# Moving operands at a pitch of 1280 bytes, and small copies on ScalarE, in a two-layer hybrid decoder trunk

## The chip, the core and the metric

The kernel runs on one core of a Trainium2 chip. The core has five engines that run their own streams of instructions and wait for each other on semaphores: TensorE (PE, matmul, with its weight loads shown as PEld), VectorE (DVE), ScalarE (ACT), GpSimd (POOL) and SyncE (SP), which here issues the DMAs. The metric is the device time of one execution in microseconds.

## The reference

Each of two layers is a half-step feed-forward block, a mixer, and a second half-step feed-forward block:

```
x = x + 0.5 * swiglu(rmsnorm(x, norm_ffn1[l]), w_ffn1_gu[l], w_ffn1_down[l])
m = mixer(rmsnorm(x, norm_mix[l]), states, w_in[l], ...)
x = x + m
x = x + 0.5 * swiglu(rmsnorm(x, norm_ffn2[l]), w_ffn2_gu[l], w_ffn2_down[l])
...
# mixer
q, k, v, g, a_lr, z, xbc, dt_raw, gate_a, gate_b = split(u @ w_in)
o_gla = gla_chunked(q, k, v, log_a, gla0)          # gated linear attention
xbc = silu(causal_dwconv(xbc, conv0))              # 4 taps, old rows from conv0
y, ssm_new = ssd_chunked(xs, dt, A, B, C, ssm0)    # h <- decay * h + dS, y_off = C . h
m = sigmoid(gate_a) * (o_gla @ w_proj_gla) + sigmoid(gate_b) * (y @ w_proj_ssm)
return m @ w_out, new states
```

There are 256 prompt tokens and 8 samples of 4 tokens, so 288 columns; the model width is 1024, the feed-forward width 2816, and the mixer has 32 state heads of 64 x 128 in 4 groups that share B and C. All of it is in 32-bit floats, and a sample's states come from memory and go back to it.

## The kernel before

Activations are held transposed, features on the partitions and the 288 columns along the free axis. A product is made of three matmuls, to keep 32-bit accuracy: weights and activations are each split into a high part in the matmul's format and the rest (wh and wl, xh and xl). `weights` (line 174) loads a block of 128 output features (wr) on the SP queue, `split` makes wh on ScalarE (line 165) and wl on VectorE (line 171). `mm3` (line 181) then runs, for each 128 rows of the contraction, wh times xh (line 184) and wh times xl (line 185), and after that wl times xh (line 187): 24 matmuls for 1024 rows. The moving operands are the normed input (xh and xl, nine buffers each, given out in turn), the feed-forward's inner activations (hh and hl), and in the mixer oh and ob (the input of w_out) and yh and yb (the input of the state branch's projection). wr has four buffers, wh and wl three each. All are of 288 floats, 1152 bytes, per partition and tile.

The order of the instructions on each engine isn't that of the code: the framework's scheduler sets it when the kernel is built. The addresses are given out by the framework too.

The mixer's second half, `ssd`, is a generator of stages that lie among blocks of the input projection. `conv` copies a block's columns into a buffer beside the old rows of the samples (line 873, GpSimd) and does the four taps (lines 876 to 878); `conv_last` saves the last rows (lines 897 and 899, GpSimd). `stage_pack` makes, for one group of heads, c4, C of the samples four times with a mask (line 928, GpSimd), and b4, a packed copy of B (`pack`, line 143, GpSimd). `stage_group` spreads c4 over the partitions with a matmul (line 939), copies it into cbd (line 942, ScalarE), and forms the products of B and C (lines 956 to 958). `stage_t` transposes a head pair's states (line 993, VectorE) and then decays them (line 998, GpSimd, eight instructions of 128 x 128 for each of 16 head pairs). `stage_h` multiplies C by the states (line 1009). `stage_y` adds the new part to the states and stores them. The POOL instructions run in one queue in the scheduler's order, so c4 can stand behind decays.

Of the kernel before, what the change touches and what calls it, by code (L numbers as in the profile page):

```python
# [23 lines left out]
NT = SEQ + NSAMP  # L24
FFN = 2816
KF = 22
# [15 lines left out]
H2_BUFS = 2  # L42
# [55 lines left out]
def tile_hybrid_step(  # L98
# [42 lines left out]
    def pack(eng, out, src):  # L141

        eng.tensor_copy(out=out.rearrange("p (r c i) -> p r c i", r=4, c=4),
                        in_=bcast(src.rearrange("p (r i) -> p r i", i=8), 2, 4))
# [4 lines left out]

    cbd = cst.tile([128, 2 * 516], F32, name="cbd")  # L150
    cz = cbd[:, 0:528].rearrange("p (a b) -> p a b", a=2)
# [61 lines left out]
    def params(l, n1):  # L213
        pa = t1()[:, 0:128]
        rows = [(norm_mix[l], 16), (norm_ffn2[l], 24), (gla_norm[l], 32),
                (ssm_norm[l], 40), (conv_b[l], 56), (norm_final, 80)]
        ds = tmp.tile([16, 2], F32, name="ds", tag="ds")
        for a, r0 in rows:
            n = a.shape[0] // 128
            nc.sync.dma_start(out=pa[r0:r0 + n], in_=a.rearrange("(r c) -> r c", c=128))  # L220
        nc.sync.dma_start(out=ds, in_=d_skip[l].rearrange("(j h) -> j h", h=2))
        V.tensor_copy(out=pa[0:16].rearrange("p (h q) -> p h q", h=2), in_=bcast(ds, 2, 64))
        pb = t1()[0:96, 0:128]
        nc.sync.dma_start(out=pb, in_=conv_w[l].rearrange("i (r c) -> (i r) c", c=128))
        p = pst()
        tr(p[:, 0:88], pa[0:88], 88)
        o = tmp.tile([128, 88], F32, name="prm", tag="prm", bufs=2)
        A.activation(out=o, in_=p[:, 0:88], func=AF.Copy)
        p = pst()
        tr(p[:, 0:96], pb, 96)  # L230
        cw = tmp.tile([128, 96], F32, name="cw", tag="cw", bufs=1)

        A.activation(out=cw, in_=p[:, 0:96], func=AF.Copy, scale=0.5)
        V.tensor_scalar(out=o[:, 32:80], in0=o[:, 32:80], scalar1=0.5, scalar2=None, op0=ALU.mult)
        a32 = tmp.tile([32, 2], F32, name="a32", tag="a32", bufs=2)
        nc.sync.dma_start(out=a32[:, 0:1], in_=dt_bias[l].rearrange("(h o) -> h o", o=1))
# [44 lines left out]
    def xpair():  # L281
        return (res.tile([128, NT], F32R, name="xh", tag="xh", bufs=9),
                res.tile([128, NT], F32R, name="xl", tag="xl", bufs=9))
# [8 lines left out]
    def ffn(norm, w_gu, w_dn, nxt, setup=False):  # L292
        with tc.tile_pool(name="ffn", bufs=1) as fp:
            hh = fp.tile([128, KF, NT], F32R, name="hh")
            hl = fp.tile([128, KF, NT], F32R, name="hl")
# [282 lines left out]
    def gla(l, P, W, norm, X, renorm, dtc, dalt, o8):  # L578
        with tc.tile_pool(name="gla", bufs=1) as gp:
            G.memset(cbd[:, 0:528], 0.0)  # L580
# [281 lines left out]
    def ssd(l, P, W, X, yf, dtm, ac, dec3, eAm, decs, mse, acd, ysq, scf, cbufs, yr, yblk, proj):  # L862
# [3 lines left out]
        with tc.tile_pool(name="ssd", bufs=1) as sp_:  # L866
            def conv(pg, cb, tag, bufs):
# [5 lines left out]
                G.tensor_copy(out=sb[:, :, 0:3], in_=scf[:, 0:24, cb].rearrange("p (s t) -> p s t", t=3))  # L873
# [34 lines left out]

            G.memset(cbd, 0.0)
# [14 lines left out]
            def stage_pack(g):  # L924
# [3 lines left out]
                G.tensor_tensor(out=c4, in0=bcast(Cf[:, sp], 1, 4), in1=bcast(C["qm"], 2, 32), op=ALU.mult)  # L928
                b4 = sp_.tile([128, 128], F32, name="b4", tag="b4", bufs=3)
                pack(G, b4, Bf[:, sp])  # L930
                R["gp", g] = Bf, Cf, c4, b4

            def stage_group(g):

                Bf, Cf, c4, b4 = R.pop(("gp", g))


                p = pst()
                T.matmul(p[:, 0:128], lhsT=C["id4"], rhs=c4.rearrange("p b t -> p (b t)"), start=True, stop=True)
                for a in range(4):  # L940
                    rows = slice(32 * a, 32 * a + 32)
                    A.activation(out=cbd[rows].rearrange("p (h x) -> p h x", x=516)[:, :, 0:512].rearrange(
                        "p h (k c) -> p h k c", c=32)[:, :, :, 8 * a:8 * a + 4],
                        in_=p[rows, 0:128].rearrange("p (k h t) -> p h k t", h=2, t=4), func=AF.Copy)
# [21 lines left out]
                ms = sp_.tile([128, 4, 32], F32, name="msm", tag="msm", bufs=2)  # L966
                G.tensor_tensor(out=ms, in0=mse[:, 4 * g:4 * g + 4], in1=bcast(cbs, 1, 4), op=ALU.mult)
# [18 lines left out]
            def stage_t(j):  # L986
# [14 lines left out]
            def stage_h(hg):  # L1001
# [9 lines left out]
                yos = sp_.tile([128, 2, 4, 32], F32, name="yos", tag="h1", bufs=3)  # L1011
# [4 lines left out]
            def stage_x(j):  # L1016
# [5 lines left out]
                pack(G, x4, xs[:, sp])  # L1022
# [36 lines left out]
            def stage_y(j):  # L1059
# [18 lines left out]
                if j % 2 == 0:  # L1078
                    R["so", j // 2] = sp_.tile([128, 2, 128], F32, name="so", tag="h1", bufs=3)
# [29 lines left out]
            stage_group(0)  # L1109
            yield 1  # L1110
            stage_x(1)
            stage_t(1)
            stage_mask(0)
            yield 1
            stage_m(0)
            stage_h(0)
            yield 1
            for j in range(16):
# [52 lines left out]
    for l in range(DEPTH):  # L1171
# [40 lines left out]
        with tc.tile_pool(name="fin", bufs=1) as op:  # L1212
            if l == DEPTH - 1:
                yo = op.tile([128, 3, D], F32, name="yo")
                rt = op.tile([128, 3], F32, name="rt")
# [46 lines left out]
```

## Time and profile before

| | us |
|---|---|
| median of 3 executions | 1842.87 |
| lowest, highest | 1842.05, 1844.18 |
| the profiled execution, its own time | 1842.29 |
| its span | 1840.5 |

| engine | busy in the span | instructions |
|---|---|---|
| PE | 98% | 14304 |
| DVE | 68% | 2091 |
| ACT | 56% | 1850 |
| POOL | 20% | 549 |

The span is what the profiler shows between the first and the last instruction; 1.8 us of the execution lie around it. Matmuls are pipelined, and one's shown duration (about 297 ns for the main ones) overlaps the next, so their pace is read from start to start. An engine's share is a mean over stages: GpSimd works almost only in the two mixers.

### The profile page before, as it was taken

To read this page: it belongs to the slowest core of one execution; us is meant where nothing else is said; L and a number is where in the kernel's file an instruction comes from. 1 tells how busy PE (TensorE), PEld (TensorE's weight loads), DVE (VectorE), ACT (ScalarE), POOL (GpSimd) and SP (SyncE) were. 2 spreads that over 40 slices of the span, in tenths; PEclk is the share of its full clock that TensorE was granted. 3 is DMA by queue.
4 is the path that set the end of the run, shared out by engine and by line. 5 is a ranking of instruction groups with operands and counts; after the bars stand their busy time and mean duration, and the time that the engine had idled before them with its cause. 6 is when DMAs were issued, how large, how long until landed. Compare 5 with 4: busy or idle time off the path is not lost.

```text
span 1840.5 us, 36290 instructions
## 1 busy us (share of the span) xinstructions
PE 1798.1 (98%) x14304; PEld 1738.7 (94%) x14304; DVE 1259.7 (68%) x2091; ACT 1023.8 (56%) x1850; POOL 376.3 (20%) x549
## 2 busy tenths in 40 slices
PE   8999999989999999999999999999899999999998
PEld 8999999889889999999999999998888999999997
DVE  6555577679898767555565556777798987665554
ACT  6444476566667646444454445665766765454443
POOL 1000000046786500000000000000577781000000
PEclk9999999999999999999999999999999999999999
DMA  7555654866687655555555555568667776555552
GB/s 217 164 168 158 164 149 125 266 183 181 190 225 221 191 168 173 163 170 161 170 164 163 165 160 161 144 177 241 174 190 214 216 209 179 170 166 162 163 163 90
DMA packets 613118, 325.59 MB, mean 177 GB/s; under 512 B 17090, under 2 KB 607858, under 8 KB 612948
## 3 DMA queue, kind: packets, MB, share of 16 engines
q1 hardware_dynamic: 612900, 323.15, 61.0%
q8 instruction: 112, 1.84, 0.4%
q14 instruction: 58, 0.48, 0.1%
q10 hardware_dynamic: 48, 0.13, 0.0%
HBM read 293.01 MB, written 30.22 MB: 176 GB/s over the span
## 4 chain that ended last, share of the span: by engine, by line
PE 52%; DVE 3%; ACT 2%; DMA 2%; POOL 1%; issue 1%; DVEq 0%; SPq 0%; POOLq 0%; ACTq 0%
PE psg L184 16%; PE psg L185 16%; PE psg L187 16%; DMA wr<-in_w_in_dram 1%; POOL st L998 1%; DVE wl L171 1%; PE pst L147 1%; ACT wh L165 1%; DMA out_dram<-st 0%; DVE cacc L878 0%; PE yo L1009 0%; PE pst L1067 0%; PE pst L1092 0%; PE pst L807 0%; PE gyo L798 0%
## 5 line engine op out<-in xcount | busy, mean ns | idle before, releaser
L165 ACT ACTIVATE wh<-wr 128x1024 fp32r<-128x1024 f32 (+1 forms) x498 | 518.6, 1042 | 509.9 <-PE psg L185 391.0
L184 PE MATMUL psg<-xh,wh 128*128 128x288 f32 x2704 | 739.4, 299 | 4.9 <-ACT cbuf L872 2.4
L185 PE MATMUL psg<-xl,wh 128*128 128x288 f32 x2704 | 735.0, 297 | 0.1
L171 DVE TENSOR_TENSOR wl<-wr,wh 128x1024 fp32r<-128x1024 f32 (+1 forms) x496 | 596.0, 1203 | 145.3 <-ACT wh L165 143.3
L184 PEld LDWEIGHTS psg<-xh,wh 128*128 128x128 f32 x2704 | 508.0, 188 | 13.6 <-ACT cbuf L872 2.8
L185 PEld LDWEIGHTS psg<-xl,wh 128*128 128x128 f32 x2704 | 508.1, 188 | 3.8 <-issue 0.9
L187 PE MATMUL psg<-xh,wl 128*128 128x288 f32 x2704 | 417.9, 297 | 3.5 <-DVE wl L171 3.4
L187 PEld LDWEIGHTS psg<-xh,wl 128*128 128x128 f32 x2704 | 379.1, 189 | 7.6 <-DVE wl L171 5.6
L998 POOL TENSOR_SCALAR st<-st,decs 128x128 f32<-128x128 f32 x256 | 237.7, 945 | 35.8 <-DVE sT L993 17.7
L184 PE MATMUL psg<-hh,wh 128*128 128x288 f32 x704 | 190.3, 296 | 0.0
L185 PE MATMUL psg<-hl,wh 128*128 128x288 f32 x704 | 189.9, 295 | 0.0
L380 POOL MEMSET cbuf<- 128x3 f32 x4 | 0.3, 108 | 654.4 <-DVE t L331 654.4
L185 PEld LDWEIGHTS psg<-hl,wh 128*128 128x128 f32 x704 | 132.7, 188 | 0.0
L184 PEld LDWEIGHTS psg<-hh,wh 128*128 128x128 f32 x704 | 132.4, 188 | 0.1
L311 DVE TENSOR_TENSOR t<-t,psg 128x288 f32<-128x288 f32 x88 | 40.0, 454 | 134.9 <-ACT wh L165 122.8
L187 PE MATMUL psg<-hh,wl 128*128 128x288 f32 x704 | 109.3, 296 | 0.0
L308 DVE TENSOR_TENSOR t<-psg,rr 128x288 f32<-128x288 f32 x88 | 40.2, 457 | 90.5 <-PE psg L187 90.5
L187 PEld LDWEIGHTS psg<-hh,wl 128*128 128x128 f32 x704 | 99.0, 188 | 0.0
L878 DVE SCALAR_TENSOR_TENSOR cacc<-cbuf,cw,cacc 128x312 f32<-128x312 f32 x144 | 78.9, 548 | 12.2 <-ACT cacc L876 11.8
L184 PE MATMUL psg<-oh,wh 128*128 128x288 f32 x256 | 69.7, 299 | 0.0
L184 PE MATMUL psg<-yh,wh 128*128 128x288 f32 x256 | 69.7, 299 | 0.0
L185 PE MATMUL psg<-ob,wh 128*128 128x288 f32 x256 | 68.9, 295 | 0.0
(317 smaller groups left out, 2248.3 us busy)
## 6 DMA issues: line engine op xcount, KB each, us to landing
wr<-in_w_ffn_gu_dram SPq DMA_DIRECT2D x176, 512.0 KB
wr<-in_w_in_dram SPq DMA_DIRECT2D x160, 512.0 KB
wr<-in_w_ffn_down_dram SPq DMA_DIRECT2D x64, 448.0 KB
wr<-in_w_ffn_down_dram SPq DMA_DIRECT2D x32, 512.0 KB
st<-in_state_ssm_dram SPq DMA_DIRECT2D x64, 256.0 KB
out_dram<-st SPq DMA_DIRECT2D x64, 256.0 KB
wr<-in_w_proj_ssm_dram SPq DMA_DIRECT2D x32, 512.0 KB
gst<-in_state_gla_dram SPq DMA_DIRECT2D x32, 256.0 KB
```

What stands on the lines that cost most here:

```text
L147: T.transpose(out, in_, ident[0:k, 0:k])
L165: A.activation(out=h, in_=raw, func=AF.Copy)
L171: V.tensor_tensor(out=lo, in0=raw, in1=h, op=ALU.subtract)
L184: T.matmul(out, lhsT=h[:, k], rhs=xh[k], start=start and k == 0, stop=False)
L185: T.matmul(out, lhsT=h[:, k], rhs=xl[k], start=False, stop=False)
L187: T.matmul(out, lhsT=lo[:, k], rhs=xh[k], start=False, stop=stop and k == n - 1)
L308: V.tensor_tensor(out=t, in0=pg, in1=r, op=ALU.mult)
L311: V.tensor_tensor(out=h, in0=t, in1=pu, op=ALU.mult)
L380: G.memset(cbufs[i][:, 0:3], 0.0)
L878: V.scalar_tensor_tensor(out=acc, in0=buf[:, i:i + NCV], scalar=w[i], in1=acc, op0=ALU.mult, op1=ALU.add)
L998: G.tensor_scalar(out=st[:, r], in0=st[:, r], scalar1=decs[:, n:n + 1], scalar2=None, op0=ALU.mult)
```

## The change

Five things change. The tiles xh, xl, hh and hl get 320 floats of which 288 are used, so that their pitch is 1280 bytes; a pad of 256 bytes and a longer rt shift what is allocated. The copy of the old conv rows, the packing and the masked C go from GpSimd to ScalarE. The decays leave `stage_t` for a stage of their own, `stage_decay`, an iteration later. The spread of C gets the bank that the product of C and the states uses (tag acc) and stands at the end of `stage_group`, which itself goes behind `stage_x(1)`. And some tiles move or lose a buffer (cbd, cz, msm, prm, h1) to make room.

```diff
+NTP = 320
...
     def pack(eng, out, src):
 
-        eng.tensor_copy(out=out.rearrange("p (r c i) -> p r c i", r=4, c=4),
-                        in_=bcast(src.rearrange("p (r i) -> p r i", i=8), 2, 4))
+        out, in_ = out.rearrange("p (r c i) -> p r c i", r=4, c=4), bcast(src.rearrange("p (r i) -> p r i", i=8), 2, 4)
+        if eng is A:
+            A.activation(out=out, in_=in_, func=AF.Copy)
+        else:
+            eng.tensor_copy(out=out, in_=in_)
...
-    cbd = cst.tile([128, 2 * 516], F32, name="cbd")
-    cz = cbd[:, 0:528].rearrange("p (a b) -> p a b", a=2)
...
     def xpair():
-        return (res.tile([128, NT], F32R, name="xh", tag="xh", bufs=9),
-                res.tile([128, NT], F32R, name="xl", tag="xl", bufs=9))
+        return (res.tile([128, NTP], F32R, name="xh", tag="xh", bufs=9)[:, 0:NT],
+                res.tile([128, NTP], F32R, name="xl", tag="xl", bufs=9)[:, 0:NT])
...
-            hh = fp.tile([128, KF, NT], F32R, name="hh")
-            hl = fp.tile([128, KF, NT], F32R, name="hl")
+            fp.tile([128, PAD], F32, name="pad")
+            hh = fp.tile([128, KF, NTP], F32R, name="hh")[:, :, 0:NT]
+            hl = fp.tile([128, KF, NTP], F32R, name="hl")[:, :, 0:NT]
...
-                G.tensor_copy(out=sb[:, :, 0:3], in_=scf[:, 0:24, cb].rearrange("p (s t) -> p s t", t=3))
+                A.activation(out=sb[:, :, 0:3], in_=scf[:, 0:24, cb].rearrange("p (s t) -> p s t", t=3), func=AF.Copy)
...
-                G.tensor_tensor(out=c4, in0=bcast(Cf[:, sp], 1, 4), in1=bcast(C["qm"], 2, 32), op=ALU.mult)
+                for b in range(4):
+                    A.activation(out=c4[:, b], in_=Cf[:, sp], func=AF.Copy, scale=C["qm"][:, b:b + 1])
                 b4 = sp_.tile([128, 128], F32, name="b4", tag="b4", bufs=3)
-                pack(G, b4, Bf[:, sp])
+                pack(A, b4, Bf[:, sp])
...
-                p = pst()
-                T.matmul(p[:, 0:128], lhsT=C["id4"], rhs=c4.rearrange("p b t -> p (b t)"), start=True, stop=True)
...
-                ms = sp_.tile([128, 4, 32], F32, name="msm", tag="msm", bufs=2)
-                G.tensor_tensor(out=ms, in0=mse[:, 4 * g:4 * g + 4], in1=bcast(cbs, 1, 4), op=ALU.mult)
+                ms = mse[:, 4 * g:4 * g + 4]
+                G.tensor_tensor(out=ms, in0=ms, in1=bcast(cbs, 1, 4), op=ALU.mult)
+
+
+                p = ps.tile([128, 128], F32, name="pc", tag="acc", bufs=1)
+                T.matmul(p[:, 0:128], lhsT=C["id4"], rhs=c4.rearrange("p b t -> p (b t)"), start=True, stop=True)
...
+
+            def stage_decay(j):
                 for hf in range(2):
                     st = R["st", j][hf]
                     for r in range(4):
...
             stage_t(0)
-            stage_group(0)
             yield 1
             stage_x(1)
+            stage_group(0)
             stage_t(1)
             stage_mask(0)
             yield 1
             stage_m(0)
+            stage_decay(0)
             stage_h(0)
...
                 if j + 2 < 16:
                     stage_t(j + 2)
+                if j + 1 < 16:
+                    stage_decay(j + 1)
```

On PE, at the spread of C of the first group in layer 0, this stands before (L939 is the spread, L147 a transpose, L956 to L958 the products of B and C, L187 matmuls of a weight block, L1009 the product with the states):

```order
L187 MATMUL psg<-xh,wl 128x288 x3
L939 MATMUL pst<-c_4405,call 128x128
L147 MATMUL pst<-call,bcf 128x128 x2
L147 MATMUL pst<-call,b_4407 128x128
L956 MATMUL pst<-bcf 128x256
L957 MATMUL pst<-bcf 128x128
L958 MATMUL pst<-bcf,b_4407 128x32
L187 MATMUL psg<-xh,wl 128x288 x5
L1009 MATMUL yo<-sT,cbd 32x64 x32
```

and this after (L967 is the spread, into pc, L151 a transpose, L954 a product, L1016 the product with the states, L185, L186 and L188 the lines of `mm3`); the two transposes of B stand 21 rows ahead of L967 and the two large products (L952, L953) three and four rows ahead of it:

```order
L188 MATMUL psg<-xh,wl 128x288 x3
L967 MATMUL pc<-c_4407,call 128x128
L151 MATMUL pst<-call,b_4412 128x128
L954 MATMUL pst<-bcf,b_4412 128x32
L188 MATMUL psg<-xh,wl 128x288 x5
L185 MATMUL psg<-xh,wh 128x288
L186 MATMUL psg<-xl,wh 128x288
L185 MATMUL psg<-xh,wh 128x288
L186 MATMUL psg<-xl,wh 128x288
L185 MATMUL psg<-xh,wh 128x288
L186 MATMUL psg<-xl,wh 128x288
L1016 MATMUL yo<-sT,cbd 32x64 x32
```

The spread is no longer the first of the group: two transposes and two products now stand ahead of it, and six more matmuls of a block stand between it and the product with the states.

On POOL, at the start of the same stage, this stands before (L998 are the decays, L897 and L899 the saving of last rows, L873 the old conv rows, L928 the masked C, L143 the packing):

```order
L998 TENSOR_SCALAR st<-st,decs 128x128 x8
L873 COPY cbuf_2523<-scf 128x8x3
L897 COPY scf<-cbuf_2523 128x3
L899 COPY scf<-cbuf_2523 128x24
L897 COPY scf<-cbuf_2524 128x3
L899 COPY scf<-cbuf_2524 128x24
L928 TENSOR_TENSOR c_4405<-bcf,call 128x128
L143 COPY b_4407<-bcf 128x128
```

and this after (L1005 are the decays, L900 and L902 the saving of last rows, L963 the mask times mse):

```order
L1005 TENSOR_SCALAR st<-st,decs 128x128 x8
L900 COPY scf<-cbuf_2523 128x3
L902 COPY scf<-cbuf_2523 128x24
L900 COPY scf<-cbuf_2524 128x3
L902 COPY scf<-cbuf_2524 128x24
L963 TENSOR_TENSOR mse<-mse,cbs 128x128
L1005 TENSOR_SCALAR st<-st,decs 128x128 x4
```

The masked C, the packing and the old rows are gone from the queue. On ACT, the same place before (L1041 a mask step, L876 a tap of the conv, L942 cbd, L950 and L952 copies of the transposes):

```order
L1041 ACTIVATE m<-acb,ac 128x128
L165 ACTIVATE wh<-wr 128x1024
L876 ACTIVATE cacc<-cbuf_2523,prm,cw 128x312
L942 ACTIVATE cbd<-pst 32x2x16x4 x4
L950 ACTIVATE bt<-pst 128x256
L952 ACTIVATE bpk<-pst 128x128
```

and after (L1048 the mask step, L933 the masked C, L146 the packing, L879 the tap, L970 cbd):

```order
L1048 ACTIVATE m<-acb,ac 128x128
L933 ACTIVATE c_4407<-bcf,call 128x32 x4
L146 ACTIVATE b_4412<-bcf 128x128
L879 ACTIVATE cacc<-cbuf_2523,prm,cw 128x312
L946 ACTIVATE bt<-pst 128x256
L948 ACTIVATE bpk<-pst 128x128
L970 ACTIVATE cbd<-pc 32x2x16x4
```

The split of a weight block (L165) that stood behind the mask steps has left this place, and the masked C and the packing have come.

## Rows read from the trace of the kernel before

**Rows 1.** The page: span, engines, the chain that ended last by engine and line.
```profile
span 1840.5 us, 36290 instructions
...
PE 1798.1 (98%) x14304; PEld 1738.7 (94%) x14304; DVE 1259.7 (68%) x2091; ACT 1023.8 (56%) x1850; POOL 376.3 (20%) x549
...
PE 52%; DVE 3%; ACT 2%; DMA 2%; POOL 1%; issue 1%; DVEq 0%; SPq 0%; POOLq 0%; ACTq 0%
PE psg L184 16%; PE psg L185 16%; PE psg L187 16%; DMA wr<-in_w_in_dram 1%; POOL st L998 1%; DVE wl L171 1%; PE pst L147 1%; ACT wh L165 1%; DMA out_dram<-st 0%; DVE cacc L878 0%; PE yo L1009 0%; PE pst L1067 0%; PE pst L1092 0%; PE pst L807 0%; PE gyo L798 0%
```

**Rows 2.** Main matmuls grouped by line: busy us, mean ns; idle before.
```profile
L184 PE MATMUL psg<-xh,wh 128*128 128x288 f32 x2704 | 739.4, 299 | 4.9 <-ACT cbuf L872 2.4
L185 PE MATMUL psg<-xl,wh 128*128 128x288 f32 x2704 | 735.0, 297 | 0.1
...
L187 PE MATMUL psg<-xh,wl 128*128 128x288 f32 x2704 | 417.9, 297 | 3.5 <-DVE wl L171 3.4
...
L184 PE MATMUL psg<-hh,wh 128*128 128x288 f32 x704 | 190.3, 296 | 0.0
```

**Rows 3.** Windows of three gate-up passes: busy (instructions) per engine, PEclk, DMA, GB/s.
```profile
30.00:110.00 80.00, 80.00 (x600) 80.00 (x599) 47.34 (x71) 40.99 (x60) 0.00 (x0) 1.00 0.57 166
720.00:800.00 80.00, 80.00 (x610) 79.82 (x609) 45.33 (x65) 38.83 (x54) 0.00 (x0) 1.00 0.57 165
1630.00:1710.00 80.00, 80.00 (x602) 80.00 (x602) 44.69 (x64) 37.64 (x51) 0.00 (x0) 1.00 0.57 166
```

**Rows 4.** Chain that ended last, inside a gate-up block: start us, us, what.
```profile
1633.04 0.14 PE psg L185
...
1633.31 0.13 PE psg L185
```

**Rows 5.** Timeline of PE: first and last main matmuls by place of the operand.
```profile
15.15 0.35 PE L185 MATMUL psg<-xl,wh 128*128 128x288 f32 x1
15.33 0.29 PE L184 MATMUL psg<-xh,wh 128*128 128x288 f32 x1
...
155.66 0.29 PE L184 MATMUL psg<-hh,wh 128*128 128x288 f32 x1
...
1615.11 0.96 PE L187 MATMUL psg<-oh,wl 128*128 128x288 f32 x6
...
1828.76 1.09 PE L187 MATMUL psg<-hh,wl 128*128 128x288 f32 x7
```

**Rows 6.** Waits: engine, line, releaser; us in total, times, longest.
```profile
PE pst L939 <- POOL c L928: 10.1, 2, 5.1
```

**Rows 7.** Timeline of layer 0 about the spread of C, all engines.
```profile
385.26 7.01 POOL L998 TENSOR_SCALAR st<-st,decs 128x128 f32<-128x128 f32 x8
...
388.89 0.28 DVE L886 SCALAR_TENSOR_TENSOR bcf<-t,cacc 128x32 f32<-128x32 f32 x1
...
389.20 1.06 ACT L165 ACTIVATE wh<-wr 128x1024 fp32r<-128x1024 f32 x1
...
393.41 0.79 PE L939 MATMUL pst<-c,call 128*128 128x128 f32 x2 [5.07 <-POOL c L928]
...
394.25 1.11 ACT L942 ACTIVATE cbd<-pst 32x128 f32<-32x128 f32 x4 [1.11 <-PE pst L939]
```

**Rows 8.** Windows of 1 us there, columns as in rows 3.
```profile
391.00:392.00 1.00, 0.00 (x0) 0.00 (x0) 0.00 (x0) 0.00 (x0) 1.00 (x3) 0.50 1.11 329
...
397.00:398.00 1.00, 1.00 (x28) 0.76 (x30) 1.00 (x4) 0.41 (x2) 0.00 (x0) 0.73 0.00 0
```

**Rows 9.** Groups of the mixer's copies on POOL and ACT, columns as in rows 2.
```profile
L873 POOL COPY cbuf<-scf 128x24 f32<-128x24 f32 x48 | 17.3, 363 | 152.1 <-ACT scf L387 106.2 <-DVE cacc L878 33.8 <-DVE cbs L965 8.6
...
L1055 ACT ACTIVATE xpk<-xd 128x128 fp32r<-128x128 f32 x32 | 9.7, 304 | 16.8 <-DVE xd L1050 16.8
L872 ACT ACTIVATE cbuf<-psg 128x32 f32<-128x32 f32 x48 | 9.4, 196 | 0.0
```

**Rows 10.** Sum of thirteen windows of 20 us, 380 to 640, by engine.
```profile
sum 260.00, PE 246.37 PEld 231.16 DVE 220.34 ACT 176.08 POOL 178.83; mean PE 18.95 PEld 17.78 DVE 16.95 ACT 13.54 POOL 13.76
```

More of the change, by code (lines that the diff above doesn't have):

```diff
@@ L41 @@
 PRE1 = 6
-H2_BUFS = 2
+PAD = 64
 ST_BUFS = 8
@@ L226, in params @@
         tr(p[:, 0:88], pa[0:88], 88)
-        o = tmp.tile([128, 88], F32, name="prm", tag="prm", bufs=2)
+        o = tmp.tile([128, 88], F32, name="prm", tag="prm", bufs=1)
         A.activation(out=o, in_=p[:, 0:88], func=AF.Copy)
@@ L579, in gla @@
         with tc.tile_pool(name="gla", bufs=1) as gp:
-            G.memset(cbd[:, 0:528], 0.0)
+            cz = gp.tile([128, 2, 264], F32, name="cz")
+            G.memset(cz, 0.0)
             cg = gp.tile([128, CONSTS.shape[1] - NKEEP], F32, name="cg")
@@ L907, in conv_store @@
                 nc.sync.dma_start(out=dst.rearrange("s i (a c) -> (s i a) c", c=128)[96 * c % 576:96 * c % 576 + n], in_=o[0:n])
+            cbd = sp_.tile([128, 2 * 516], F32, name="cbd")
             G.memset(cbd, 0.0)
@@ L935, in stage_group @@
                 Bf, Cf, c4, b4 = R.pop(("gp", g))
-                p = pst()
-                T.matmul(p[:, 0:128], lhsT=C["id4"], rhs=c4.rearrange("p b t -> p (b t)"), start=True, stop=True)
[L940 to L944, printed above, removed]
                 p = pst()
@@ L965, in stage_group @@
                 V.tensor_tensor(out=cbs, in0=p[:, 384:416], in1=C["btc"], op=ALU.mult)
-                ms = sp_.tile([128, 4, 32], F32, name="msm", tag="msm", bufs=2)
-                G.tensor_tensor(out=ms, in0=mse[:, 4 * g:4 * g + 4], in1=bcast(cbs, 1, 4), op=ALU.mult)
+                ms = mse[:, 4 * g:4 * g + 4]
+                G.tensor_tensor(out=ms, in0=ms, in1=bcast(cbs, 1, 4), op=ALU.mult)
+                p = ps.tile([128, 128], F32, name="pc", tag="acc", bufs=1)
+                T.matmul(p[:, 0:128], lhsT=C["id4"], rhs=c4.rearrange("p b t -> p (b t)"), start=True, stop=True)
+                for a in range(4):
+                    rows = slice(32 * a, 32 * a + 32)
+                    A.activation(out=cbd[rows].rearrange("p (h x) -> p h x", x=516)[:, :, 0:512].rearrange(
+                        "p h (k c) -> p h k c", c=32)[:, :, :, 8 * a:8 * a + 4],
+                        in_=p[rows, 0:128].rearrange("p (k h t) -> p h k t", h=2, t=4), func=AF.Copy)
                 R["g", g] = bt, bpk, cb3, ms
@@ L1010, in stage_h @@
                                      start=hf == 0 and b == 0, stop=hf == 1 and b == 3)
-                yos = sp_.tile([128, 2, 4, 32], F32, name="yos", tag="h1", bufs=3)
+                yos = sp_.tile([128, 2, 4, 32], F32, name="yos", tag="h1", bufs=2)
                 V.tensor_tensor(out=yos, in0=bcast(yo.rearrange("p (j q) -> p j q", j=2), 2, 4),
@@ L1021, in stage_x @@
                 x4 = sp_.tile([128, 128], F32, name="b4", tag="b4", bufs=3)
-                pack(G, x4, xs[:, sp])
+                pack(A, x4, xs[:, sp])
                 acb = sp_.tile([128, 2, SEQ], F32, name="acb", tag="acb", bufs=2)
@@ L1078, in stage_y @@
                 if j % 2 == 0:
-                    R["so", j // 2] = sp_.tile([128, 2, 128], F32, name="so", tag="h1", bufs=3)
+                    R["so", j // 2] = sp_.tile([128, 2, 128], F32, name="so", tag="h1", bufs=2)
                 so = R["so", j // 2]
@@ L1214, in tile_hybrid_step @@
                 yo = op.tile([128, 3, D], F32, name="yo")
-                rt = op.tile([128, 3], F32, name="rt")
+                rt = op.tile([128, 64], F32, name="rt")[:, 0:3]
                 G.memset(rt, 1.0)
```

## The prediction

> **What bounds the kernel now.** I read the page first. TensorE (PE) is busy 98% of a span of 1840.5 us and the chain that ended last is half PE's own instructions, with nothing else above 3% [rows 1]. The reader should see that there are two kinds of time to win: PE's own pace, and the few places where PE waits. The pace matters because of a count: lines 184, 185 and 187 run 2,704 times each on xh and xl, and line 184 704 times on hh, with 185 and 187 as often [rows 2], so 3 x 2,704 + 3 x 704 = 10,224 matmuls use the operands whose pitch changes. A nanosecond on each is 10.2 us.
>
> Next I asked whether they all cost the same. Four gate-up passes run the same stream of instructions, yet in windows of 80 us without a wait at a granted clock of 1.00 they start 600, 610 and 602 matmuls [rows 3]: 133.3, 131.1 and 132.9 ns each. What differs between the passes is only which of the nine xh and xl buffers stand where. The chain inside one block shows it at work: steps of the same line 185 take 0.13 and 0.14 us in turn [rows 4]. So I sorted the start-to-start intervals of the main matmuls (those under 200 ns) by the address of the moving operand, taken from the compiled allocation. At 1152 bytes, 4.5 x 256, successive tiles alternate between two places modulo 256, while every weight tile stands at 0 modulo 256. Operands at 0 modulo 256 take 131.66 ns (4,337 intervals, first at 15.33, last at 1829.28 in the row of 1828.76), at 128 they take 134.59 ns (3,975, first at 15.15, last at 1829.41), at 96 and 224 they take 132.87 and 132.57 ns (1,406 each, from 155.66 and 155.92 to 1615.64 and 1615.78) [rows 5]. The mean over the operands that change is 133.0 ns. The cost rises with the distance to 0, counted round the circle of 256; since all weights stand at 0, this trace can't tell distance from the weights from distance to 0.
>
> Last come the waits. PE's longest single wait is that for the masked C (c4), 10.1 us in two waits, one in each layer [rows 6].
>
> **The change part by part.** *Pitch.* 1280 is 5 x 256, so tiles no longer alternate. In the compiled allocation of the changed kernel all weights, xh, xl, hh and hl stand at 224 modulo 256: 0 from the weights, 224 in absolute terms. If distance from the weights counts, every changed interval goes from 133.0 to about 131.5 ns (131.66 for those at 0; 131.35 for 1,576 intervals whose predecessor is at 0 too): 1.5 x 10,224 = 15.3 us. If the absolute place counts, it goes to 132.6 ns, 0.4 x 10,224 = 4 us, or nothing. The Trainium skill ("SBUF — State Buffer", section "Who interferes with whom") speaks against this edit: it gives PE two independent read ports, one for the moving operand and one for weights, and lets only VectorE and GpSimd contend. By it placement is free and this term would be 0; identical passes at 133.3 and 131.1 ns don't agree with that. I take 15.3, because the difference between passes is as large and is tied to the buffers alone, and I keep 0 for the range.
>
> *Masked C and the bank.* In layer 0, VectorE finishes C at 388.89 + 0.28 = 389.17. The c4 on POOL stands behind eight decays of the state (7.01 us from 385.26), so PE, done at 388.34, waits 5.07 us [rows 7]. While it waits the granted clock falls to 0.50, and it is still 0.73 on average between 397 and 398 [rows 8]; from 393.41 to about 397.5 PE works at the lower level, 1.2 GHz, and so loses about half of 4.1 us, 2.1 us. Gross: 7.2 us in a layer.
>
> After the change c4 is four ScalarE pieces. ScalarE has the three mask steps until 389.3, then 4 x 0.2 us (line 872, the same 32 columns, takes 196 ns [rows 9]): c4 at about 390.1. The order puts the transposes of B and two products ahead of the spread, so PE comes to the spread at about 388.9 and waits 1.2 us; b4 comes about 0.3 later; the state matmuls behind wait for four cbd copies (1.11 us for four [rows 7]), partly under eleven matmuls that now stand between, which leaves about 1.0. So 2.5 us remain in short pieces, during which I expect the clock to stay up. Net 7.2 - 2.5 = 4.7 in a layer, **9.4 us** in two. The bounds are 14.4 (no wait left) and 0 (other waits in the same stage take all of it back).
>
> *ScalarE for GpSimd.* POOL loses 48 copies of old conv rows (17.3 us), 40 packings and 8 masked C. ScalarE gains 48 x 0.2 + 40 x 0.3 (line 1055's 304 ns for 128 columns) + 32 x 0.2 = 28 us [rows 9], spread over two mixers. In 380 to 640 us ScalarE is busy 176 of 260 us [rows 10], so 14 us per layer fit, and VectorE at 220 is nearer to its limit and gets none. A weight split (line 165) that starts at 389.20 today [rows 7] moves behind the masks of B, but its block is used only several us later. POOL's relief may shorten some waits (about 18 us of the chain is POOL's decays [rows 1], c4 among them), ScalarE's load may lengthen some: I take +3 against -3.
>
> *Decays an iteration later.* 256 decays stay 256; they leave the way of conv_last and c4, but each state tile is decayed nearer to the matmul result that is added to it on VectorE. An iteration is about 15 us and eight decays 7, so they fit; nothing.
>
> *The rest* costs nothing: cbd and cz change pools, and their memsets stand before long POOL idleness; msm is written in place into mse, whose slice nobody else reads; h1 with two buffers makes the copy of so wait for a store issued an iteration before, and yos for matmuls already passed. The loads on the SP queue stay as they are.
>
> **Sum** against the profiled execution's own 1842.3 us: -15.3 - 9.4 = 1817.6. The median, 1842.87, is 0.6 above that execution, so **1818 us**.
>
> **The rivals.** *R1, placement earns nothing* (only the absolute place counts, or pairs of operands that I haven't sorted): 1842.9 - 9.4 = 1833.5, down to 1829.5 with the 4 us of the 224 row. For it: all weights stand at one place, so distance was never tried. (The skill's rule of independent ports, above, ends here.) Against it: the pattern round the circle is centred just where the weights are. 25%.
>
> *R2, the new place is the costly one*, the side slower than before. If with everything at 224 the two reads meet each time and the interval becomes the 134.5 ns of today's 128, the term is +1.5 x 10,224 = +15.3 and the time 1842.9 + 15.3 - 9.4 = 1849. It decides from a mean above 133.0 + 9.4/10.2 = 133.9 ns. For it: moving the weights off 0 moves something that was never varied. Against it: 96 and 224 cost the middle value, not the high one. 10%.
>
> *R3, a bigger gain*: with all operands alike, each interval falls to what operands at 0 take in the window of 720 to 800 [rows 3], 129.5 ns (304 intervals from 720.05 to 799.89; the 301 at 128 there take 132.9): 3.5 x 10,224 = 36 us, 1842.9 - 36 - 9.4 = 1797. For it: the place modulo 256 doesn't explain why this pass is quicker in both classes. Against it: three of four passes don't show it. 9%. The Trainium skill ("TensorE: Matmul & The Clock Gate", section "Wait — 56ns, not 53.3ns?") gives a matmul of N columns N/2.4 + 2.5 ns, here an estimate of 122.5; by it the time would be near 1735, and no interval class here comes near it.
>
> *R4, ScalarE is late*: the pieces added in the mixer push the weight splits, PE waits for wh in that stage, and the 9.4 us go back; 1842.9 - 15.3 = 1827.6. It needs about 5 us of new waits per layer against 84 us of ScalarE idleness in 260. 6%.
>
> **How the numbers follow.** My forecast, with the sum as it stands, has 50%. R1 has 25%, R2 10%, R3 9%, R4 6%. The forecast, R1 and R4 hold 81%; from R3's near end, 1797, to R1's upper end with half of the masked C's gain taken back, 1833.5 + 4.5 = 1838, is the range. No change within 0.2% (3.7 us, about what a measurement of this kernel can tell) comes about where R1 meets a lost c4 gain, or R2 in a milder form: 5%. Slower is the rest of R2, 9%; faster 86%.
>
> **What would show it.** Right: gate-up windows of 80 us with 608 to 610 matmuls in every pass, and line 185's steps all alike in the chain; no wait over 2 us before line 967 (spread of C, now into pc), and PEclk 1.00 about 390 to 398. Wrong: passes that still differ (R1), 595 in each window (R2), 618 (R3), or PE waiting for wh (line 166) and cbuf in 380 to 640 us (R4). What would make the prediction wrong above all is the unknown that carries most of the sum: whether the matmul's cost follows distance from the weights.

## The result and the profile after

The changed kernel takes 1818.12 us (median of four executions, 1817.65 to 1818.64) against 1843.02 for the kernel before: a ratio of 0.9865, interval 0.9848 to 0.9882. The forecast of 1818 us is met, and so is the direction. The two terms of its sum are each off by about 2 us, in opposite directions, so the closeness is partly luck; the experiments show where.

The page of the changed kernel; lines 185, 186 and 188 are now what 184, 185 and 187 were in [rows 2]:

```profile
span 1816.6 us, 36201 instructions
...
PE 1781.6 (98%) x14304; PEld 1722.5 (95%) x14304; DVE 1257.0 (69%) x2091; ACT 1042.3 (57%) x1970; POOL 349.0 (19%) x453
...
L185 PE MATMUL psg<-xh,wh 128*128 128x288 f32 x2704 | 731.9, 298 | 8.9 <-ACT cbuf L875 4.9
L186 PE MATMUL psg<-xl,wh 128*128 128x288 f32 x2704 | 727.7, 296 | 0.1
```

The span is 23.9 us shorter. The shares hardly move, since PE is still the bound; GpSimd has 96 instructions less and ScalarE 120 more. What one matmul costs can't be read from these means, because their ends overlap; the windows of the four gate-up passes show it (columns as in [rows 3]):

```profile
30.00:110.00 80.00, 80.00 (x610) 80.00 (x609) 47.89 (x73) 41.55 (x60) 0.00 (x0) 1.00 0.59 169
720.00:800.00 80.00, 80.00 (x608) 79.82 (x607) 45.33 (x65) 38.27 (x52) 0.00 (x0) 1.00 0.57 167
915.00:995.00 80.00, 80.00 (x611) 80.00 (x610) 47.88 (x69) 40.68 (x57) 0.00 (x0) 1.00 0.57 166
1610.00:1690.00 80.00, 80.00 (x610) 80.00 (x609) 44.30 (x63) 38.51 (x51) 0.00 (x0) 1.00 0.57 166
```

Where [rows 3] had 600, 610 and 602, all passes now start 608 to 611 in 80 us. From start to start the 9,898 undisturbed intervals of the changed operands take 131.74 ns, against 133.01 before.

At the spread of C in layer 0, where [rows 7] had the wait of 5.07 us, the timeline of all engines reads:

```profile
381.86 7.33 POOL L1005 TENSOR_SCALAR st<-st,decs 128x128 f32<-128x128 f32 x8
...
386.39 0.27 DVE L889 SCALAR_TENSOR_TENSOR bcf<-t,cacc 128x32 f32<-128x32 f32 x1
...
386.52 0.70 PE L952 MATMUL pst<-bcf 128*128 128x256 f32 x2 [1.50 <-DVE bcf L885]
...
386.76 0.95 ACT L933 ACTIVATE c<-bcf,call 128x32 f32<-128x32 f32 x4
...
387.81 0.45 PE L967 MATMUL pc<-c,call 128*128 128x128 f32 x2
...
390.24 1.10 PE L1016 MATMUL yo<-sT,cbd 128*32 128x64 f32 x64 [0.20 <-POOL scf L902]
```

The eight decays run as long as ever, until 389.2, but nothing that PE wants stands behind them: ScalarE makes c4 from 386.76 and the spread follows at 387.81 without a wait. (The 0.20 us before line 1016 are put down to GpSimd's saved rows, but that product reads cbd, whose last copy on ScalarE ends at 390.14.) PE now waits 1.50 us for VectorE's C itself, and the granted clock stays at its upper level through that wait, where [rows 8] had 0.50 (windows of 1 us):

```profile
385.00:386.00 1.00, 0.03 (x1) 0.00 (x0) 1.00 (x1) 1.00 (x7) 1.00 (x2) 1.00 1.12 335
386.00:387.00 1.00, 0.48 (x2) 0.45 (x3) 0.67 (x3) 1.00 (x6) 1.00 (x2) 1.00 1.18 295
387.00:388.00 1.00, 1.00 (x10) 0.95 (x9) 0.00 (x0) 1.00 (x6) 1.00 (x3) 1.00 1.21 290
```

PE's waits after show what is left: the wait of [rows 6] is gone, and the longest of the mixer is now one of 2.9 us at line 185.

```profile
PE psg L185 <- ACT cbuf L875: 4.9, 2, 2.9
...
PE pst L952 <- DVE bcf L885: 2.5, 2, 1.5
```

To see where the time went, I took the start of the same main matmul in both traces (the one at 372 us in the kernel before, and so on) and compared the stretches between. "All" runs from the first main matmul to the last, "outside" is all but the two state stages, "spread" the stretches 372 to 420 and 1280 to 1330 where C is first spread, "rest" the remainder of the state stages to 640 and 1545. The change in us against the profiled execution of before, for each kernel of this study, and last the time in which the granted clock stood at the lower level, 0.50, up to the last main matmul (before: 17.1 us):

```
               outside  spread   rest    all   at 0.50
changed           -8.8    -9.6   -5.6  -24.0       3.4
shift128          -9.0    -9.7   -5.8  -24.5       6.8
pitch1152          2.7    -9.2   -4.7  -11.3      10.2
dist128            2.4   -10.1   -3.8  -11.4       3.4
dist64            -5.9    -8.4   -6.0  -20.3      13.7
pitch1152_d64     -0.9   -10.0   -8.4  -19.4       0.0
dist32             2.4   -11.1   -2.8  -11.5       6.8
dist192            4.6    -9.7   -4.7   -9.7       6.8
pitch_only        -8.6     0.0    4.3   -4.3      20.5
c4_act             0.3    -2.0    1.3   -0.3      17.1
c4_pool           -7.0    -1.5    0.9   -7.7      23.9
rows_pool         -5.1    -7.1   -5.2  -17.5      10.2
spread_back       -7.6    -9.7   -3.2  -20.6      10.2
```

These are single profiled executions; differences of 1 to 2 us among them mean nothing by themselves. Part of them is the clock. 3.4 us at the lower level with PE busy cost about half of that, 1.7 us (an estimate from the two levels), and such stretches come and go between kernels of one and the same order: `shift128` has one from 1363.3 that the changed kernel lacks, `pitch1152` one from 1166.4 and one from 1374.6.

### The profile page after: what moved, and what is told of

Its sections match the earlier page's. It is cut to its first block, busy times and chain, and to the rows that moved or that the text cites. A ratio compares the mean times of both kernels' runs of the same rounds, so it can differ in the third digit from the quotient of the medians.

```text
span 1816.6 us, 36201 instructions
## 1 busy us (share of the span) xinstructions
PE 1781.6 (98%) x14304; PEld 1722.5 (95%) x14304; DVE 1257.0 (69%) x2091; ACT 1042.3 (57%) x1970; POOL 349.0 (19%) x453
## 4 chain that ended last, share of the span: by engine, by line
PE 52%; DVE 3%; ACT 3%; DMA 2%; POOL 1%; issue 1%; DVEq 0%; ACTq 0%; POOLq 0%
PE psg L185 16%; PE psg L188 16%; PE psg L186 16%; DMA wr<-in_w_in_dram 2%; DVE wl L172 1%; POOL st L1005 1%; PE pst L151 1%; ACT wh L166 1%; DVE sT L998 0%; PE pst L1074 0%; PE pst L1099 0%; ACT bm L979 0%; PE pst L810 0%; DVE cacc L881 0%; PE yo L1016 0%
## 5 line engine op out<-in xcount | busy, mean ns | idle before, releaser
L185 PE MATMUL psg<-xh,wh 128*128 128x288 f32 x2704 | 731.9, 298 | 8.9 <-ACT cbuf L875 4.9
L186 PE MATMUL psg<-xl,wh 128*128 128x288 f32 x2704 | 727.7, 296 | 0.1
L185 PEld LDWEIGHTS psg<-xh,wh 128*128 128x128 f32 x2704 | 507.4, 188 | 18.6 <-ACT cbuf L875 5.8
L186 PEld LDWEIGHTS psg<-xl,wh 128*128 128x128 f32 x2704 | 507.4, 188 | 3.9 <-issue 0.9
L188 PE MATMUL psg<-xh,wl 128*128 128x288 f32 x2704 | 415.3, 295 | 0.2
L188 PEld LDWEIGHTS psg<-xh,wl 128*128 128x128 f32 x2704 | 375.8, 188 | 2.4 <-issue 0.9
L1005 POOL TENSOR_SCALAR st<-st,decs 128x128 f32<-128x128 f32 x256 | 241.9, 964 | 41.8 <-DVE sT L998 33.9
L185 PE MATMUL psg<-hh,wh 128*128 128x288 f32 x704 | 188.8, 294 | 0.0
L186 PE MATMUL psg<-hl,wh 128*128 128x288 f32 x704 | 188.3, 294 | 0.0
L185 PEld LDWEIGHTS psg<-hh,wh 128*128 128x128 f32 x704 | 132.1, 188 | 0.1
L186 PEld LDWEIGHTS psg<-hl,wh 128*128 128x128 f32 x704 | 132.1, 188 | 0.0
L313 DVE TENSOR_TENSOR t<-t,psg 128x288 f32<-128x288 f32 x88 | 39.9, 454 | 132.8 <-ACT wh L166 119.5
L188 PE MATMUL psg<-hh,wl 128*128 128x288 f32 x704 | 108.3, 294 | 0.0
L188 PEld LDWEIGHTS psg<-hh,wl 128*128 128x128 f32 x704 | 98.1, 188 | 0.0
L185 PE MATMUL psg<-oh,wh 128*128 128x288 f32 x256 | 69.9, 300 | 0.0
L185 PE MATMUL psg<-yh,wh 128*128 128x288 f32 x256 | 69.7, 299 | 0.0
L186 PE MATMUL psg<-ob,wh 128*128 128x288 f32 x256 | 69.1, 295 | 0.0
```

Of the source, the lines that this page charges most:

```text
L185: T.matmul(out, lhsT=h[:, k], rhs=xh[k], start=start and k == 0, stop=False)
L186: T.matmul(out, lhsT=h[:, k], rhs=xl[k], start=False, stop=False)
L188: T.matmul(out, lhsT=lo[:, k], rhs=xh[k], start=False, stop=stop and k == n - 1)
L313: V.tensor_tensor(out=h, in0=t, in1=pu, op=ALU.mult)
L1005: G.tensor_scalar(out=st[:, r], in0=st[:, r], scalar1=decs[:, n:n + 1], scalar2=None, op0=ALU.mult)
```

## The experiments

**Pitch or moved work.** `pitch1152` undoes the pitch alone; every engine has the same instructions in the same order as in the changed kernel, only addresses differ.

```diff
-NTP = 320
+NTP = 288
```

> The changed kernel with the pitch of xh, xl, hh and hl back at 1152 bytes (NTP = 288) and all else kept; the order of instructions is the same row for row. Theory (cost follows the distance of the operand from the weights modulo 256): the operands alternate between distance 0 and 128, the mean interval rises from 131.7 to about 133.1 ns, 1.35 x 10,224 = 14 us, so 1832 us. Rival (the gain came from the moved work alone and pitch only looks tied to it): 1818 us.

Measured: 1831.94 us, ratio to before 0.9931 (0.9912 to 0.9951). Its intervals take 133.11 ns, and its gate-up passes differ again, as those of [rows 3] do:

```profile
30.00:110.00 80.00, 80.00 (x600) 80.00 (x600) 47.74 (x72) 41.23 (x59) 0.00 (x0) 1.00 0.58 167
720.00:800.00 80.00, 80.00 (x610) 79.82 (x610) 44.72 (x64) 38.37 (x52) 0.00 (x0) 1.00 0.58 168
```

The theory's number holds: the addresses alone are worth 14 us in the changed kernel. But not all of it is pace. The executions have granted clocks of 0.994 to 0.996, those of the changed kernel and of `shift128` 0.995 to 0.998, and the difference of the means makes 3 to 4 us. In the table 11.5 us of the 12.7 lie outside the state stages, where 7,876 of the 10,224 matmuls stand; the other 2,348, at 1.37 ns each, would give 3.2 us and show 1.3.

The distance doesn't explain one pass against another. In the pass at 720 the operands that take turns start 610, no fewer than the changed kernel's 608. Sorted by address as in the prediction, those at distance 0 take 133.3, 129.4, 131.6 and 131.0 ns in `pitch1152` in the passes at 30, 720, 915 and 1630, and within 0.2 of that before; those at 128 cost more than those at 0 in each pass. What sets the level of a pass with mixed places stays open.

**Distance, place or pitch.** Four kernels keep the pitch of 1280 and the order, and put a pad between the weights and the operands (`dist32`, `dist64`, `dist128`, `dist192`) or ahead of both (`shift128`).

The first line is that of `dist128` (16 floats in `dist64`, 8 in `dist32`, 48 in `dist192`), the second that of `shift128`:

```diff
+    call = cst.tile([128, NKEEP], F32, name="call"); res.tile([128, 32], F32, name="padx")
...
+    call = cst.tile([128, NKEEP], F32, name="call"); cst.tile([128, 32], F32, name="padc")
```

The pads move every tile that is allocated behind them, not the operands alone; that it's the operands rests on the sorting within one trace, above and in the prediction. `dist192` gets its room from two small tiles made one and a buffer less for a 32-byte tile, and PAD is 72 there; the weights stand at 192 instead of 224 modulo 256.

> The changed kernel, pitch 1280, with a pad of 128 bytes between the weights and the operands: all moved operands stand at distance 128 from the weights; order the same row for row. Theory (distance from the weights): every interval like today's at 128, about 134.3 ns, +2.6 x 10,224 = 27 us, so 1845 us, slower than the kernel before. Rival (it is the pitch, or that all operands stand alike, and not the distance): 1818 us.

> The changed kernel with a pad of 128 bytes ahead of the weights: weights and operands move together to 96 modulo 256, distance stays 0; order the same row for row. Theory (distance): 1818 us, nothing changes. Rival (the absolute place counts): the intervals become those of 96 in the kernel before, 132.9 ns, +1.1 x 10,224 = 12 us, so 1830 us.

> The same with a pad of 64 bytes, distance 64, where no mean was measured for whole passes. Theory (cost rises with the distance round the circle): about 132.7 ns, +1.0 x 10,224 = 10 us, so 1828 us. Rival (only the same half of 256 bytes, or the pitch, counts): 1818 us.

`shift128` takes 1817.58 us (0.9855, interval 0.9833 to 0.9876), the changed kernel's time, with 131.74 ns. So the absolute place is out. `dist128` takes 1831.63 us (0.9934, 0.9910 to 0.9957): the pitch of 1280 is worth nothing at that distance, and that the operands stand alike isn't what counts. But it isn't 1845: all operands at 128 take 133.41 ns, not the 134.3 expected. Its windows show the cost in every pass:

```profile
30.00:110.00 80.00, 80.00 (x603) 80.00 (x602) 47.27 (x70) 41.28 (x59) 0.00 (x0) 1.00 0.58 167
720.00:800.00 80.00, 80.00 (x601) 79.81 (x600) 44.25 (x62) 37.48 (x52) 0.00 (x0) 1.00 0.57 165
```

`dist64` takes 1823.38 us (0.9885, 0.9864 to 0.9905) with 131.98 ns, not 132.7: cheaper than expected by the intervals, though still 5.8 us above `shift128`. 0.24 x 10,224 = 2.5 us of that is in the intervals. Most of the rest is the clock: the four executions have 0.994 to 0.996, those of `shift128` 0.995 to 0.997, in the mean 0.0018 less, 3.2 us. The profiled one falls to the lower level twice where `shift128` doesn't, once outside and once at the second spread (windows of 2 us, the first two of `dist64`, the third of `shift128` at the place of the first):

```profile
1160.00:1162.00 2.00, 2.00 (x10) 2.00 (x9) 0.16 (x2) 0.14 (x1) 0.00 (x0) 0.51 1.07 270
1283.00:1285.00 2.00, 2.00 (x10) 2.00 (x10) 1.88 (x4) 2.00 (x10) 2.00 (x2) 0.54 0.89 266
...
1158.00:1160.00 2.00, 2.00 (x17) 2.00 (x17) 0.70 (x5) 1.12 (x2) 0.00 (x0) 1.00 1.03 270
```

The intervals left the shape of the cost in doubt, and three more kernels followed.

> The changed kernel with a pad of 32 bytes, distance 32. Theory (flat near 0, rising beyond 64): 131.7 to 132.0 ns, 1818 to 1821 us. Rival (0 is a point of its own, any offset costs the same): 132.0 ns and 1823 us as at distance 64.

> The changed kernel with the pitch back at 1152 bytes and a pad of 64 bytes between weights and operands, so that tiles alternate between distances 64 and 192 (64 round the other way) instead of 0 and 128; order the same row for row. Theory (distance round the circle alone counts, pitch not): both places cost what 64 does, 131.98 ns, so about 132.1 ns and the 1823 us of the run at distance 64, with no longer pitch and 8 KB less memory. Rival (alternating tiles cost as such): 133.1 ns and 1832 us as at pitch 1152.

`dist32` takes 1831.42 us (0.9940, 0.9925 to 0.9954) with 133.42 ns: neither of the two expectations; distance 32 costs as much as 128. Its window:

```profile
30.00:110.00 80.00, 80.00 (x603) 80.00 (x602) 47.17 (x70) 41.24 (x59) 0.00 (x0) 1.00 0.59 167
```

`pitch1152_d64` takes 1830.11 us (0.9935, 0.9918 to 0.9952) with 132.79 ns, between the theory's 132.1 and the rival's 133.1 (its profiled execution was the quickest of the four, 1823.72, at a granted clock of 0.998; the others, at 0.994 to 0.996, lie at 1830 to 1832).

> The changed kernel, pitch 1280, with a pad of 192 bytes between weights and operands (room for it comes from one tile for two small constants and one buffer less of a 32-byte tile): distance 192 for all. Distances 32 and 128 both gave 133.4 ns, 0 gave 131.7 and 64 gave 132.0, so a cost that rises round the circle is out. Theory A (192 is as 64, and tiles that alternate cost something as such, which would explain 132.8 ns at 64 and 192 in turn): 132.0 ns, 1821 to 1823 us. Theory B (192 is a costly place, 133.6 ns, and alternating costs nothing: mean of 132.0 and 133.6 is 132.8): 1831 to 1833 us.

`dist192` takes 1833.11 us (0.9943, 0.9924 to 0.9962) with 133.35 ns: theory B. Its window:

```profile
30.00:110.00 80.00, 80.00 (x603) 80.00 (x602) 47.77 (x72) 41.23 (x60) 0.00 (x0) 1.00 0.58 167
```

So the mean interval is 131.7 at distance 0, 133.4 at 32, 132.0 at 64, 133.4 at 128 and 133.4 at 192. It depends on the place of the operand relative to the weights, but not as a slope round a circle. Taking turns between 0 and 128 costs 133.1, half a ns above the mean of the two; taking turns between 64 and 192 costs 132.8, 0.1 above it.

**The moved work alone undone.** `pitch_only` keeps pitch and memory and puts the moved instructions back; PE has the order of before. Two places of its diff against the changed kernel; packing also goes back to GpSimd, the decays into `stage_t` and the spread to its old place and bank.

```diff
-                A.activation(out=sb[:, :, 0:3], in_=scf[:, 0:24, cb].rearrange("p (s t) -> p s t", t=3), func=AF.Copy)
+                G.tensor_copy(out=sb[:, :, 0:3], in_=scf[:, 0:24, cb].rearrange("p (s t) -> p s t", t=3))
...
-                for b in range(4):
-                    A.activation(out=c4[:, b], in_=Cf[:, sp], func=AF.Copy, scale=C["qm"][:, b:b + 1])
+                G.tensor_tensor(out=c4, in0=bcast(Cf[:, sp], 1, 4), in1=bcast(C["qm"], 2, 32), op=ALU.mult)
...
```

> The changed kernel with every moved instruction put back (masked C, packing and old rows on GpSimd, decays in stage_t, spread of C first in its group and in its old bank, stage_group(0) before stage_x(1)); pitch and memory layout stay. PE's order is that of the kernel before. Theory (pitch and moved work add up): the intervals give 13.0 us, so 1830 us, and the 5.07 us wait at the spread of C with its fall of the clock is there again. Rival (the moved work is worth nothing by itself, the pitch gives all): 1818 us. Rival (the pitch alone gives nothing in the old order, since the mixer takes it back): 1840 us.

Measured: 1836.21 us (median of ten, 1831.51 to 1839.99; 0.9960, 0.9946 to 0.9975), between the theory and the second rival. Outside the state stages it gains 8.6 us, the changed kernel 8.8, and the 5 us wait is back (POOL's c now at line 932). But the rest of the state stages is 4.3 us slower than before although each matmul is quicker: the pace gives 1,822 x 1.27 ns = 2.3 us there, but PE is idle 4.9 us longer (the gaps over 0.15 us of the two traces), and one more stretch at the lower clock costs 1.7. Of PE's waits:

```profile
PE pst L941 <- POOL c L932: 10.0, 2, 5.0
PE psg L185 <- ACT cbuf L875: 5.6, 2, 2.9
```

The longest of the second row is at 1380.04 in layer 1. The same block waited 1.22 us before and waits 2.91 in the changed kernel (the third line):

```profile
1383.90 0.40 PE L184 MATMUL psg<-xh,wh 128*128 128x288 f32 x1 [1.22 <-ACT cbuf L872]
...
1380.04 0.40 PE L185 MATMUL psg<-xh,wh 128*128 128x288 f32 x1 [2.88 <-ACT cbuf L875]
...
1365.25 0.40 PE L185 MATMUL psg<-xh,wh 128*128 128x288 f32 x1 [2.91 <-ACT cbuf L875]
```

Behind the wait of `pitch_only` stand the loads: ScalarE's split waits for a weight block,

```profile
1376.40 1.06 ACT L166 ACTIVATE wh<-wr 128x1024 fp32r<-128x1024 f32 x1 [4.25 <-DMA wr<-in_w_in_dram]
```

while the DMA engines are full and, after PE has been idle for 2.88 us, the clock falls to its lower level (windows of 2 us; the last three columns are clock, DMA share and GB/s):

```profile
1376.00:1378.00 2.00, 1.16 (x9) 0.93 (x8) 0.51 (x1) 1.06 (x1) 1.35 (x5) 1.00 1.17 292
1378.00:1380.00 2.00, 0.00 (x0) 0.00 (x0) 1.06 (x3) 1.77 (x4) 0.05 (x1) 1.00 1.19 283
...
1382.00:1384.00 2.00, 2.00 (x10) 2.00 (x9) 2.00 (x5) 0.47 (x1) 0.00 (x0) 0.50 0.05 12
```

So at this place a burst of loads and state transfers ends last, not PE, and a quicker matmul only waits longer; other places weren't followed back to their loads. (Whether the memory edits that come with the pitch add to it wasn't tried apart.)

**The masked C alone, each way.** `c4_act` is the kernel before with c4 and the packing of B on ScalarE; `c4_pool` is the changed kernel with c4 back on GpSimd (the c4 lines of the diff above, taken backwards for the one and as they stand for the other).

> The kernel before with one edit: masked C (c4) and the packing of B on ScalarE. Theory (the wait for c4 behind the decays, with the clock, is nearly all that the moved work gives): wait at the spread under 2 us, clock 1.00 there, about 9 us less, 1834 us. Rival (the relief of GpSimd's queue by old rows and packing matters as much): 5 us less, 1838 us. Rival (ScalarE late): 1843 us.

> The changed kernel with the masked C alone back on GpSimd; packing, old rows, the late spread in the bank of C.h stay. Theory (c4 stands behind the decays): PE waits again some 4 to 5 us in each layer and the clock falls, +9 us, 1827 us. Rival (the late spread with its bank covers it): 1818 to 1820 us.

`c4_act` takes 1841.55 us (0.9991, 0.9978 to 1.0004), hardly a gain, and 2.0 us at the spread; the theory had 1834. `c4_pool` takes 1834.70 us (0.9953, 0.9935 to 0.9971), 16.6 us above the changed kernel and 8 above the theory's 1827. 8.1 of them lie at the spread, where PE waits for c4 again and the clock is at 0.50 for 6.8 us in each layer, and 6.5 in the rest of the state stages:

```profile
PE pc L966 <- POOL c L932: 5.2, 2, 2.7
```

The masked C on ScalarE is necessary, then, and not sufficient. (In these kernels and the next two the scheduler also places other instructions anew, in `c4_pool` 116 on PE.) ScalarE's rows in `c4_act` tell why:

```profile
390.05 0.95 ACT L932 ACTIVATE c<-bcf,call 128x32 f32<-128x32 f32 x4
390.89 0.31 ACT L145 ACTIVATE b<-bcf 128x128 f32<-128x128 f32 x1
393.25 0.65 ACT L879 ACTIVATE cacc<-cbuf,prm,cw 128x312 f32<-128x312 f32 x1 [2.05 <-POOL cbuf L876]
393.80 1.09 ACT L946 ACTIVATE cbd<-pst 32x128 f32<-32x128 f32 x4
```

and GpSimd's, what it waits for:

```profile
384.85 8.19 POOL L1002 TENSOR_SCALAR st<-st,decs 128x128 f32<-128x128 f32 x8
392.99 0.23 POOL L876 COPY cbuf<-scf 128x24 f32<-128x24 f32 x1
```

c4 is ready early, but the conv's tap on ScalarE waits for the old rows, which stand behind the same eight decays on GpSimd, and the cbd copies stand behind the tap. PE's wait has moved from the spread to the product with the states, and the clock falls there as it did before:

```profile
PE yo L1013 <- ACT cbd L946: 4.8, 2, 2.4
...
PE pst L943 <- ACT c L932: 1.9, 2, 1.0
...
397.00:398.00 1.00, 1.00 (x4) 1.00 (x5) 1.00 (x3) 1.00 (x5) 0.51 (x1) 0.50 0.00 0
```

**Old rows and packing of x back on GpSimd** (`rows_pool`, from the changed kernel):

```diff
-                A.activation(out=sb[:, :, 0:3], in_=scf[:, 0:24, cb].rearrange("p (s t) -> p s t", t=3), func=AF.Copy)
+                G.tensor_copy(out=sb[:, :, 0:3], in_=scf[:, 0:24, cb].rearrange("p (s t) -> p s t", t=3))
...
-                pack(A, x4, xs[:, sp])
+                pack(G, x4, xs[:, sp])
```

> The changed kernel with the old conv rows and the packing of x back on GpSimd (80 instructions off ScalarE); masked C and the packing of B stay on ScalarE. Theory (these two edits cost and give nothing): 1817 to 1820 us. Rival (they free GpSimd's queue, on which the conv waits): +4 us, 1822 us. Rival (ScalarE's load hurts): 1815 us.

Measured: 1823.14 us (0.9892, 0.9873 to 0.9911), 5 us above the changed kernel: the rival, though its interval overlaps that of the changed kernel. In the profile it is 6.5: 2.5 us stand at the spread, where the tap waits again, 0.4 in the rest of the state stages, and 3.7 outside, where the trace has two stretches at the lower clock that the changed kernel lacks (from 262.9 and 1160.6, about 3.4 us):

```profile
391.92 0.65 ACT L879 ACTIVATE cacc<-cbuf,prm,cw 128x312 f32<-128x312 f32 x1 [1.83 <-POOL cbuf L876]
```

**The late spread undone** (`spread_back`, from the changed kernel): the spread and its copies stand first in `stage_group` again, with a bank of tag t, and `stage_group(0)` ahead of `stage_x(1)`.

```diff
                 p = pst()
+                T.matmul(p[:, 0:128], lhsT=C["id4"], rhs=c4.rearrange("p b t -> p (b t)"), start=True, stop=True)
...
-                p = ps.tile([128, 128], F32, name="pc", tag="acc", bufs=1)
...
             stage_t(0)
+            stage_group(0)
             yield 1
             stage_x(1)
-            stage_group(0)
```

> The changed kernel with the spread of C put back first in its group, in a bank of tag t, and stage_group(0) back ahead of stage_x(1); masked C, packing and old rows stay on ScalarE, pitch 1280. Theory (the edits at this place need each other; the late spread covers what remains of ScalarE's time): 2 to 4 us of wait return in each layer, 1822 to 1826 us. Rival (masked C on ScalarE suffices): 1818 to 1820 us.

Measured: 1822.20 us (0.9897, 0.9876 to 0.9917), inside the theory's range, but not for its reason: at the spread it gains the same 9.7 us as the changed kernel. So with the old rows on ScalarE the late spread isn't needed there; with the rows on GpSimd, `rows_pool` (-7.1) against `c4_act` (-2.0) suggests that it covers part of the wait. The 4 us (3.4 in the profile), again with intervals that overlap, are in the rest of the state stages (2.4) and outside (1.2). Outside, the trace has a stretch at the lower clock from 1158.1, about 1.7 us; in the rest PE is idle as long as in the changed kernel (11.4 us) and the clock as low, so what holds the 2.4 stays open.

**The late decays.** With `stage_decay` folded back into `stage_t` in the changed kernel, the scheduler puts out the same instructions in the same order on all five engines. Beside the other edits this one moves nothing.

## Why the prediction was right, and where it was not

*Pitch.* That the pace follows the place relative to the weights is shown by `shift128` and `dist128` against the changed kernel; why it does isn't shown. The Trainium skill gives the moving operand and the weights independent read ports ("SBUF — State Buffer", section "Who interferes with whom"). What the prediction drew from that, that placement is free, the runs don't bear out: `shift128` and `dist128`, of one order and one pitch, lie 14 us apart. Three parts of the step fell. "The cost rises with the distance to 0, counted round the circle of 256" is wrong: 32 costs what 128 does, and 64 nearly what 0 does. The means of places that take turns don't carry over to a place alone: 128 took 134.59 ns in the trace before and takes 133.41 in `dist128`. And the term was 15.3, with an interval of 131.5 and all 10,224 matmuls; measured are 131.74 ns and 13.0 us by intervals, 12.7 from the first main matmul to the last against `pitch1152`, 13.8 by medians, of the last two some 3 to 4 by the clock. The 2,348 matmuls in the state stages hand on little of their pace. R1, R2 and R3 are out: 1833.5 asked that the place be worth nothing, R2 that the new one be costly, and no pass of the changed kernel has R3's 129.5 ns (618 in a window).

*Masked C and the clock.* 9.4 us were forecast at the two spreads, 9.6 were measured there, with the clock at 1.00 as expected. It doesn't stay up in every execution: in `dist64`, of the same order, it falls at the second spread (the window at 1283 above). The division of the remaining 2.5 us was off: PE waits 1.50 us for C, and the cbd copies are hidden but for 0.20. The step that failed is what the gain was put down to: c4 on ScalarE by itself gives 2.0, because the old rows stood behind the same decays. That edit, costed among the copies, carries the gain too: with it, `spread_back` gains the 9.7.

*ScalarE for GpSimd.* Costed at +3 against -3. In the rest of the state stages the moved work gives 4.7 us with the old pitch. This is the mis-sized term, put at nothing. Which of the moved edits earns it isn't shown: `c4_pool` loses 6.5 us in the rest, 1.7 of them by the clock, `rows_pool` only 0.4, and GpSimd's relief wasn't parted from ScalarE's load. ScalarE is busy 189 of 260 us there, against 176 in [rows 10]:

```profile
sum 260.00, PE 251.45 PEld 236.38 DVE 224.66 ACT 189.15 POOL 163.58; mean PE 19.34 PEld 18.18 DVE 17.28 ACT 14.55 POOL 12.58
```

R4 is out by the time. Of its signs, PE waits only 0.3 us in all for wh (line 166), but 4.9 for cbuf where it was 2.4; as `pitch_only` has 5.6 with no work moved, that isn't ScalarE's load.

*Sum.* 12.7 for the pitch and 11.3 for the moved work in the old pitch (9.2 and 4.7, less 2.7 outside) make the 24.0 of the table, as they must, since `pitch1152` is the kernel between. 15.3 + 9.4 = 24.7 met it because one term was 2.6 too large and the other 1.9 too small; that they cancel is luck. The parts don't add in any order: alone on the old schedule, pitch gives 4.3 in the profile and 8 by medians, since in the state stages longer waits and the clock take its gain back.

## What to carry to other kernels

Where one instruction runs ten thousand times, sort its start-to-start intervals by address: passes of the same stream that start 600 and 610 of them in the same time pointed to 14 us here, and a pad of a few dozen bytes between weights and operands is enough to win or lose them; try several distances, since one good and one bad don't give the curve. When work is taken out from behind a long job on an in-order queue, look for everything that its consumer's queue still has behind the same job; moving one of two such instructions only moved the wait. A quicker matmul gives little in a stage where PE waits for others, so take the gain per instruction only where the windows show PE without waits. And before differences of 2 to 5 us between executions are put down to an edit, compare their granted clocks: 0.001 of the mean is about 1.8 us here.

## What was not expected of the hardware

With the order of instructions the same, the mean interval of a 288-column matmul at 2.4 GHz was 131.7, 133.4, 132.0, 133.4 and 133.4 ns at distances of 0, 32, 64, 128 and 192 bytes (modulo 256) between moving operand and weights. Moving both together by 128 bytes changed nothing (131.74). Why 64 is cheap and 32 is dear stays open; so does why taking turns between 0 and 128 costs half a ns more than the mean of both, and why one pass of four with such turns ran at 131.1 ns, quicker than with all operands at 0.
